# An encoder trunk whose activations are given by feature: transposes, squares of rows and reloads taken out of its first stages

## The chip, the cores and the metric

The kernel runs on one core of one Trainium2 chip. The metric is the device time of one execution in microseconds (us). The profile is one execution seen by the hardware profiler; its clock starts at the first instruction of the program. PE is the matrix engine, ACT the scalar engine, DVE the vector engine, POOL the general engine, SP the engine that issues nearly all loads and stores; a name with a q behind it (SPq) is the engine's instruction queue.

## The reference

One encoder layer over 256 tokens of width 2048, all in float32. What the change touches is the beginning:

```python
h = rms_norm(x, norm_mix_g)           # x * rsqrt(mean(x*x) + eps) * gain, along the 2048 features
proj = h @ w_in                       # feeds retention and the gated delta rule, which follow
...
mem_n = rms_norm(mem, norm_mem_g)     # 256 memory tokens of width 2048
k, v = jnp.split(mem_n @ w_kv, 2, axis=-1)   # for the cross-attention, later in the layer
```

The rest of the layer (two token mixers merged by gates, an output projection with the residual x, cross-attention into k and v, a squared-ReLU MLP, a last norm) is not changed in what it computes. Tables that depend on positions and on the decay parameters (rotations, decays per head, decays of the retention) are also computed at the start.

## The kernel before

**How a product is made.** Every weight matrix is streamed once from memory. `fetch` (line 89) loads 1 MB of it as float32 into a ring of three buffers (`raw`), rounds it on ACT in two halves to the fast matrix format (`whi`, line 108) and has DVE subtract what was rounded off (`wlo`, line 111). Both rings hold three halves. Activations are held the same way, as a rounded part and a remainder, four feature blocks of 128 to a "quad". A product is three matrix products: rounded by rounded, rounded by remainder, remainder by rounded. `chunk` (line 137) makes 256 tokens by 512 columns out of four fetches, with 96 products of 512 columns (lines 151 to 153); one half of a fetch feeds 12 of them. `blocks` (line 177) makes two blocks of 128 features by 256 tokens out of two fetches, with a pair of products (512 and 256 columns, lines 193 and 194) for each; one half of a fetch feeds eight pairs. `narrow` (line 204) makes a product of 32 columns.

**The start, in program order.** `values(0)` to `values(3)` (lines 334, 348, 377, 530, 532) are four chunks: the memory tokens by the value half of `w_xkv`. Memory is loaded in rows of tokens, four quarters of 512 features. For each quarter `load_mem` (line 325) has PE transpose sixteen 128x128 pieces two at a time into PSUM (`to_feature`, line 255, transpose on line 262) and ACT and DVE multiply by the gain and split (lines 275, 276). The scale of each token is taken from sums of squares of the rows (ACT, line 291) and multiplied in when a chunk's result is read out of PSUM (`evac_kv`, line 337). After `values(0)`, x is loaded in rows too, its squares are summed, its scale is spread over the partitions by a small product (`scale_row`, line 299), and 32 further transposes (line 364) turn it into the quads `h1`; the transposed x is also written to a scratch tensor `xt_d` (line 368), which the output projection's residual reads back. The gains come through two transposes (line 248), the convolution weights through two more (line 386). The angles for rotation (lines 402 to 428) are a chain on DVE with two table changes on ACT. After `values(2)` comes the `narrow` product, which gives the raw decays; `decay_rows` (line 455) works them up on DVE to `cl` (line 482), which is written to memory (`crow`, line 483) and read back spread over the partitions (`row`, line 509). PE transposes the rest (line 500) and DVE copies it to `bcol` (line 501). Then `decays` (line 512) makes the tables: DVE adds a mask (`em`, line 516, two buffers), ACT takes 12 exponentials of 64 columns for each pair of heads (`dec_w`, line 521), SP stores them (line 522). `ret_decays` (line 524) makes one table a head with one exponential (`dm_w`, line 526) and one store (line 527).

**The K stage.** The loop at line 539 runs `blocks` eight times over the key half of `w_xkv`; each result is multiplied by the memory scale `mrow` into `ko` (line 543) and stored. It has 32 halves of a fetch. The decay tables are made beside it. After it, the space of all these tiles is given to the mixers, which stream `w_in`.

**What sets the order.** The program is recorded in program order with priorities, and a scheduler then puts each engine's instructions in one fixed order. On the chip each engine goes through its own list strictly in order; an instruction that waits holds up all that stand behind it. Weights have a high priority, so their loads, roundings and subtractions stand early. `step` (line 80) runs one piece of a generator from the list `steps` at fixed places inside `chunk` and `blocks`; before the change only the delta rule uses it. `issue_after(i)` puts what is issued under it no earlier in the lists than instruction i.

Of the kernel before, what the change touches and what calls it, by code (L numbers as in the profile page):

```python
# [47 lines left out]
MAGIC = 1.5 * 2.0**23  # L48


@with_exitstack
def trunk(ctx: ExitStack, tc: tile.TileContext, x, mem, positions, norm_mix_g, w_in, conv_w, gdn_a_log, gdn_dt_bias,
          ret_gn_g, gdn_norm_g, w_out, norm_x_g, norm_mem_g, w_xq, w_xkv, w_xo, norm_ffn_g, w_ff1, w_ff2,
          norm_final_g, inv_freq, out):
# [21 lines left out]
    rushed = []  # L76

    fetched, steps = [], []
# [10 lines left out]
    def fetch(pieces, k, n, rush=False, hold=None, at=(0, 0)):  # L89

# [3 lines left out]
        with tc.high_priority(offset=100000):  # L94
            for off, ap in pieces:
                src = ap.rearrange("(k p) n -> p k n", p=P)
                for ks in ((slice(0, k // 2), slice(k // 2, k)) if rush else (slice(0, k),)):
                    fetched.append(nc.sync.dma_start(rv[:, ks, off:off + ap.shape[1]], src[:, ks, :]).ins)
            got = []
            for i in range(2):  # L100
# [7 lines left out]
                rounding = act.activation(hi, src, AF.Copy)  # L108
                if rush and not i:
                    rushed.append(rounding.ins)  # L110
                vec.tensor_sub(lo, src, hi.bitcast(F32))  # L111
                got.append((hi.rearrange("p (k n) -> p k n", n=n), lo.rearrange("p (k n) -> p k n", n=n)))
        return got
# [23 lines left out]
    def chunk(quads, pieces_of, evac, before=None, hold=None):  # L137

# [16 lines left out]
        for q in range(4):  # L155
            if q not in held:
                if before and q:
                    before(q)
                halves = fetch(pieces_of(q), 4, 512, rush=before is not None and q == 0)
# [66 lines left out]
    vec.memset(warm, 0.0)  # L226
    act.activation(warm, warm, AF.Exp)
    ident = cp.tile([P, P], F32, name="ident")
    ones = cp.tile([P, P], F32, name="ones")
    vec.memset(ones, 1.0)  # L230
# [9 lines left out]
    gains = cp.tile([P, 64], F32, name="gains")  # L240

    def load_gains(c0, vectors):
        rows = sm.tile([48, P], F32, name="grow", tag="junk", bufs=1)
        n = 16 * len(vectors)
        for i, g in enumerate(vectors):
            nc.sync.dma_start(rows[16 * i:16 * (i + 1), :], g.rearrange("o (k p) -> (o k) p", p=P))
        gps = bank()
        pe.transpose(gps[:, :n], rows[:n], ident[:n, :n])
        vec.tensor_copy(gains[:, c0:c0 + n], gps[:, :n])

    with tc.high_priority(offset=200000):
        load_gains(0, (norm_mem_g,))
    G_MEM, G_MIX, G_X, G_FFN = 0, 16, 32, 48

    def to_feature(src, gain, quad):

        for f2 in range(2):
# [8 lines left out]
            qh, ql = quad  # L266
            if gain is None:
                h, l = qh[:, f2 * 2:f2 * 2 + 2, :], ql[:, f2 * 2:f2 * 2 + 2, :]
                act.activation(h, pv, AF.Copy)
                vec.tensor_sub(l, pv, h.bitcast(F32))  # L270
            else:
                for f in range(2):
                    k = f2 * 2 + f
                    g = gains[:, gain + k:gain + k + 1]
                    last = act.activation(qh[:, k, :], pv[:, f, :], AF.Copy, scale=g)  # L275
                    vec.scalar_tensor_tensor(ql[:, k, :], pv[:, f, :], g, qh[:, k, :].bitcast(F32),
                                             op0=ALU.mult, op1=ALU.subtract)
        return None if gain is None else last.ins

    def rms_cols(name, ssq, count=D):  # L280

# [25 lines left out]
    def load_rows(c, src, rush, pieces=1):  # L307
        xc = kv.tile([P, NT, 512], F32, name="xc", tag="xc", bufs=8)
        rows = src[0, :, c * 512:(c + 1) * 512].rearrange("(t p) d -> p t d", p=P)
        with tc.high_priority(offset=rush):  # L310
            for ts in (slice(i * NT // pieces, (i + 1) * NT // pieces) for i in range(pieces)):
                nc.sync.dma_start(xc[:, ts, :], rows[:, ts, :])  # L312
# [812 lines left out]
```

## Time and profile before

| | us |
|---|---|
| three runs | 2080.16, 2080.26, 2081.82 (median 2080.26) |
| the profiled execution, first to last instruction | 2078.0 |
| median less that span | 2.3 |

Only the span of the profiled execution is recorded, not a time of its own; the 2.3 us beside it lie before its first and after its last instruction. Product records on PE are listed longer than the distance between their starts, since they overlap, and a PE that waits inside a stretch of products may be listed as busy. So stretches of the timeline are read by their length and the number of products in them.

### The profile page before, as it was taken

Reading aid. Unit: us, or ns where it says so; the run is one execution under the profiler, and the core shown is the slowest. Engines: PE = TensorE matmul, PEld = TensorE weight load, DVE = VectorE, ACT = ScalarE, POOL = GpSimd, SP = SyncE. Lnnn points to the kernel's source line nnn. Section 1 sums busy time; section 2 is a strip of 40 time slices with the busy share of each in tenths; the row PEclk is TensorE's granted clock in tenths of the full one; section 3 lists DMA queues with packets and bytes.
Section 4 is the critical chain, followed back from the end, with each engine's and each line's share of the span. In section 5 each row is a group of like instructions: output and inputs, shape, how many; then the busy total and the mean of one; then the engine's idle time right before and its main releaser. Section 6 shows DMA issues by size and latency. Waiting matters only on the chain.

```text
span 2078.0 us, 28543 instructions
## 1 busy us (share of the span) xinstructions
PE 2060.9 (99%) x10996; PEld 1776.8 (86%) x10996; DVE 1404.6 (68%) x2230; ACT 1115.2 (54%) x1835; POOL 30.9 (1%) x37
## 2 busy tenths in 40 slices
PE   8999999999999999999999999999999999999998
PEld 6788888888888888888888899888888888888887
DVE  5766779778757885778557665776556556645655
ACT  7584664675547554655446554654444434434444
POOL 0000000000000000000000000000000000000000
PEclk9999999999999999999999999999999999999999
DMA  8787655556555655555467664579566656556653
GB/s 300 237 274 249 197 188 195 169 177 195 187 163 190 192 181 163 190 187 191 146 213 244 190 190 153 183 204 242 185 200 185 199 185 196 188 199 186 195 190 142
DMA packets 331064, 407.21 MB, mean 196 GB/s; under 512 B 35232, under 2 KB 239024, under 8 KB 330800
## 3 DMA queue, kind: packets, MB, share of 16 engines
q1 hardware_dynamic: 330640, 404.87, 61.1%
q8 instruction: 86, 1.41, 0.3%
q10 hardware_dynamic: 288, 0.52, 0.1%
q14 instruction: 50, 0.41, 0.1%
HBM read 389.61 MB, written 13.65 MB: 194 GB/s over the span
## 4 chain that ended last, share of the span: by engine, by line
PE 95%; DMA 2%; ACT 1%; SPq 1%; DVE 1%; issue 0%; POOLq 0%; POOL 0%; ACTq 0%; DVEq 0%
PE s L193 33%; PE s L194 17%; PE s L152 13%; PE s L153 13%; PE s L151 13%; PE b L709 1%; PE b L616 1%; DMA xc<-x 1%; ACT whi L108 1%; PE b L742 1%; PE b L122 0%; PE b L121 0%; DVE wlo L111 0%; PE b L123 0%; DMA xt_d<-xt 0%; SPq L312 0%
## 5 line engine op out<-in xcount | busy, mean ns | idle before, releaser
L111 DVE TENSOR_TENSOR wlo<-raw,whi 128x1024 fp32r<-128x1024 f32 x700 | 855.5, 1223 | 510.2 <-ACT whi L108 503.8
L108 ACT ACTIVATE whi<-raw 128x1024 fp32r<-128x1024 f32 x700 | 740.6, 1059 | 688.0 <-PE s L153 338.9
L193 PE MATMUL s<-q,whi 128*128 128x512 f32 x3072 | 1056.6, 390 | 0.3 <-DVE q L1006 0.3
L194 PE MATMUL s<-q,wlo 128*128 128x256 f32 x3072 | 839.6, 281 | 0.7 <-DVE wlo L111 0.7
L193 PEld LDWEIGHTS s<-q,whi 128*128 128x128 f32 x3072 | 567.5, 188 | 109.9 <-DVE q L1006 0.5
L194 PEld LDWEIGHTS s<-q,wlo 128*128 128x128 f32 x3072 | 576.2, 188 | 14.4 <-DVE wlo L111 2.6
L152 PE MATMUL s<-wlo,q 128*128 128x512 f32 x1264 | 495.8, 392 | 0.7 <-DVE wlo L111 0.7
L153 PE MATMUL s<-whi,q 128*128 128x512 f32 x1264 | 492.1, 390 | 0.0
L151 PE MATMUL s<-whi,q 128*128 128x512 f32 x1264 | 451.2, 390 | 2.6 <-ACT q L275 2.6
L151 PEld LDWEIGHTS s<-whi,q 128*128 128x128 f32 x1264 | 237.2, 188 | 51.8 <-ACT q L275 3.0
L152 PEld LDWEIGHTS s<-wlo,q 128*128 128x128 f32 x1264 | 237.6, 188 | 49.3 <-DVE wlo L111 2.1
L153 PEld LDWEIGHTS s<-whi,q 128*128 128x128 f32 x1264 | 237.8, 188 | 47.5
L200 ACT ACTIVATE bo<-s 128x256 f32<-128x256 f32 x192 | 72.9, 379 | 121.1 <-PE s L194 107.9
L201 DVE TENSOR_TENSOR bo<-bo,s 128x256 f32<-128x256 f32 x192 | 79.9, 416 | 44.0 <-ACT bo L200 43.7
L569 DVE SCALAR_TENSOR_TENSOR acc<-bo,cw,acc 128x255 f32<-128x255 f32 (+1 forms) x144 | 66.8, 479 | 3.1 <-ACT acc L566 1.2
L678 DVE TENSOR_TENSOR pr<-lw,tw 32x31 f32<-32x31 f32 (+15 forms) x124 | 40.5, 326 | 11.1 <-DMA lw<-scr_l 9.1
L680 DVE TENSOR_TENSOR tw<-tw,pr 32x31 f32<-32x31 f32 (+15 forms) x124 | 40.6, 327 | 2.0
L843 ACT ACTIVATE gth<-s 128x512 f32<-128x512 f32 x32 | 19.0, 594 | 21.6 <-PE s L153 15.1
L1053 DVE SCALAR_TENSOR_TENSOR res<-s,rstd3q,res 128x512 f32<-128x512 f32 (+1 forms) x32 | 22.3, 735 | 12.0 <-PE s L153 12.0
L1040 DVE SCALAR_TENSOR_TENSOR hs<-bo 128x256 f32<-128x256 f32 x64 | 26.9, 421 | 1.1
L1043 DVE TENSOR_TENSOR q<-hs,q 128x256 fp32r<-128x256 f32 x64 | 26.6, 417 | 0.0
L1042 ACT ACTIVATE q<-hs 128x256 fp32r<-128x256 f32 x64 | 26.1, 409 | 0.4 <-DVE hs L1040 0.4
(304 smaller groups left out, 1075.6 us busy)
## 6 DMA issues: line engine op xcount, KB each, us to landing
raw<-w_in SPq DMA_DIRECT2D x143, 1024.0 KB
raw<-w_ff SPq DMA_DIRECT2D x128, 1024.0 KB
raw<-w_xkv SPq DMA_DIRECT2D x31, 1024.0 KB
raw<-w_out SPq DMA_DIRECT2D x16, 1024.0 KB
raw<-w_xq SPq DMA_DIRECT2D x16, 1024.0 KB
raw<-w_xo SPq DMA_DIRECT2D x16, 1024.0 KB
dec_d<-dec_w SPq DMA_DIRECT2D x8, 384.0 KB
dec<-dec_d SPq DMA_DIRECT2D x8, 384.0 KB
```

The lines of the kernel that those rows point to most:

```text
L108: rounding = act.activation(hi, src, AF.Copy)
L111: vec.tensor_sub(lo, src, hi.bitcast(F32))
L151: pe.matmul(o, xh, wh, start=first, stop=False)
L152: pe.matmul(o, xh, wl, start=False, stop=False)
L153: pe.matmul(o, xl, wh, start=False, stop=last)
L193: pe.matmul(ps[b], lh, xhl, start=kk == 0, stop=False)
L194: pe.matmul(ps[b][:, :S], ll, xh, start=False, stop=kk == KT - 1)
L200: act.activation(o, ps[b][:, S:], AF.Copy)
L201: vec.tensor_add(o, o, ps[b][:, :S])
L569: vec.scalar_tensor_tensor(acc[:, d:], ps[:, :S - d], cw[:, j, blk:blk + 1], acc[:, d:], op0=ALU.mult, op1=ALU.add)
L678: vec.tensor_mul(pv, lw[:, j, j + 1:32].unsqueeze(2).to_broadcast([32, n, j + 1]), tw[:, j, 0:j + 1].unsqueeze(1).to_broadcast([32, n, j + ...
L680: vec.tensor_sub(tw[:, j + 1:32, 0:j + 1], tw[:, j + 1:32, 0:j + 1], pv)
```

## The change

- x and memory are given as `x_f` and `mem_f`, by feature: 128 partitions, 16 feature blocks, 256 tokens. The four norm gains (`gains_f`) and a table `small_f` (convolution weights, one gain, frequencies, two decay parameters) are laid out ahead of the launch too. The 68 transposes of memory, x, gains and convolution weights fall away, and so do the store to `xt_d`; the residual reads `x_f`.
- Sums of squares are taken from features: ACT squares 128x1024 four times, DVE adds, and two products by a column of ones sum over partitions (`norm_of`). The memory scale is no longer needed in `values`; the attention multiplies it into the values it reads back, and `ko` is multiplied by it as before.
- The first fetch is cut into four loads of 256 KB and the second into two, and a load of memory of matching size stands behind each (`along`). Roundings are cut likewise.
- Eight products of ones (`WARM`) stand at the head of PE's list.
- The squares, scale and normalization of x become a generator in `steps`, run inside `values(1)` and `values(2)`; those of memory run inside `values(3)`. All are issued under `behind`, that is, no earlier than the latest load, rounding and subtraction of weights.
- The rotations move from before `values(2)` to behind `values(3)`, and the tables of the retention from the beginning into the K stage, behind the latest weights there.
- In the last gate chunk the first fetch is cut in two loads.

In the changed kernel's lists, around the decay tables: SP has a store of `dm_w` between the store of `crow` and the loads of `row`. ACT has, between the roundings of the K stage's halves 8 and 9, a table load and the sine; between 9 and 10 a table load, a `dm_w`, a table load and the cosine; between 11 and 12 a table load and 20 `dec_w`; between 12 and 13 eleven `dec_w` and the copy of the memory scale's row. DVE has `cl` behind the subtraction of half 6; two `em`, the first step of the memory scale and `bcol` between those of halves 9 and 10; one `em` behind those of halves 10 and 11, and behind 11 two `ko` also. PE has the products for the memory scale's row inside half 9. (Before: `cl` behind half 2, two `em` behind half 4, 19 `dec_w` behind half 6, no table load, and the scale's row in half 2.)

```diff
+    @contextmanager
+    def behind():
+        with ExitStack() as orders:
+            for ins in latest.values():
+                orders.enter_context(tc.issue_after(ins))
+            yield
...
-    def fetch(pieces, k, n, rush=False, hold=None, at=(0, 0)):
+    def fetch(pieces, k, n, cuts=1, along=None, hold=None, at=(0, 0)):
...
-                for ks in ((slice(0, k // 2), slice(k // 2, k)) if rush else (slice(0, k),)):
+                for c in range(cuts):
+                    ks = slice(c * k // cuts, (c + 1) * k // cuts)
                     fetched.append(nc.sync.dma_start(rv[:, ks, off:off + ap.shape[1]], src[:, ks, :]).ins)
+                    if along:
+                        along[0](ks)
...
-                rounding = act.activation(hi, src, AF.Copy)
-                vec.tensor_sub(lo, src, hi.bitcast(F32))
+                part = k * n // max(cuts, 2)
+                for c in range(0, k * n // 2, part):
+                    cs = slice(c, c + part)
+                    latest["hi"] = act.activation(hi[:, cs], src[:, cs], AF.Copy).ins
+                    if along:
+                        along[1](slice(i * k // 2 + c // n, i * k // 2 + (c + part) // n))
+                    latest["lo"] = vec.tensor_sub(lo[:, cs], src[:, cs], hi[:, cs].bitcast(F32)).ins
...
+        early = bank()
+        for _ in range(WARM):
+            pe.matmul(early[:, :P], ones, ones, start=True, stop=True)
...
+    def norm_of(name, xfs):
+        for c, xf in enumerate(xfs):
+            sq = kv.tile([P, 4, S], F32, name="sq", tag="sq" if c else "sqa", bufs=1)
+            with behind():
+                act.activation(sq, xf, AF.Square)
+                if c:
+                    vec.tensor_add(acc, acc, sq)
+                else:
+                    acc = sq
+            if c % 2:
+                yield
...
+        for t in range(NT):
+            pe.matmul(sps[:, t:t + 1], acc[:, 0, t * P:(t + 1) * P], ones[:, :1], start=True, stop=True)
...
+        rsqrt(r, s)
+        yield
+        yield r, scale_row(f"{name}_row", r)
...
+        def load(ks):
+            nc.sync.dma_start(xf[:, ks], mem_f[:, 4 * c + ks.start:4 * c + ks.stop])
+        def rounded(ks):
+            qh, ql = memq[c]
+            for k in range(ks.start, ks.stop):
+                g = gains[:, G_MEM + 4 * c + k:G_MEM + 4 * c + k + 1]
+                act.activation(qh[:, k, :], xf[:, k], AF.Copy, scale=g)
+                vec.scalar_tensor_tensor(ql[:, k, :], xf[:, k], g, qh[:, k, :].bitcast(F32), op0=ALU.mult, op1=ALU.subtract)
...
-        chunk(memq, cols(w_xkv[0], D + n * 512), evac_kv, before=load_mem if n == 0 else None)
+        chunk(memq, cols(w_xkv[0], D + n * 512), evac_kv, cuts=1 if n else 4, along=None if n else memory)
...
+        for c in range(4):
+            for k2 in range(2):
+                with behind():
+                    xn = kv.tile([P, 2, S], F32, name="xn", tag="xn", bufs=2)
+                    for f in range(2):
+                        k = 2 * k2 + f
+                        vec.scalar_tensor_tensor(xn[:, f, :], xfs[c][:, k, :], gains[:, G_MIX + 4 * c + k:G_MIX + 4 * c + k + 1], got[1], op0=ALU.mult, op1=ALU.mult)
+                    split([a[:, 2 * k2:2 * k2 + 2, :] for a in h1[c]], xn)
+                yield
...
+    steps.append(normalized())
     values(1)
...
     values(2)
+    finish_steps()
     narrow(h1, w_in[0], C_GA, 32, decay_rows)
+    steps.append(memory_norm())
     values(3)
+    finish_steps()
+    rstdm, mrow = scales
+    with behind():
+        rotations()
     row4 = [rows_of(g) for g in range(4)]
...
-        ret_decays(b2)
+        with behind():
+            ret_decays(b2)
...
-        split(vv, vr)
+        for t in range(NT):
+            r = rstdm[:, t:t + 1]
+            act.activation(vv[0][:, t], vr[:, t], AF.Copy, scale=r)
+            vec.scalar_tensor_tensor(vv[1][:, t], vr[:, t], r, vv[0][:, t].bitcast(F32), op0=ALU.mult, op1=ALU.subtract)
```

More of the change, by code (lines that the diff above doesn't have):

```diff
@@ L238, in rsqrt, with to_feature @@
         pool.tensor_tensor(o, i, nhalf_pow[:, :o.shape[1]], op=ALU.pow)
[L240 to L252, printed above, removed]
     G_MEM, G_MIX, G_X, G_FFN = 0, 16, 32, 48
-    def to_feature(src, gain, quad):
+    def to_feature(src, quad):
         for f2 in range(2):
@@ L265, in to_feature @@
                 continue
[L266 to L280, printed above, removed]
[L282 to L287 removed]
+            split([a[:, f2 * 2:f2 * 2 + 2, :] for a in quad], pv)
     def square_sum(acc, src):
@@ L548, in trunk @@
             decays(2 + b2)
-        ret_decays(b2)
+        with behind():
+            ret_decays(b2)
     kvs.close()
```

225 lines of the change are left out of this document (101 added, 124 removed).

## The prediction

> **What bounds the kernel now.** I read the page first, then the stretches of the timeline cut at the first product of each stage, then the timeline of the first 20 us, and last the chain of work that ended last with the lists of ACT, DVE and SP around the decay tables.
>
> ```profile
> span 2078.0 us, 28543 instructions
> PE 2060.9 (99%) x10996; PEld 1776.8 (86%) x10996; DVE 1404.6 (68%) x2230; ACT 1115.2 (54%) x1835; POOL 30.9 (1%) x37
> PE 95%; DMA 2%; ACT 1%; SPq 1%; DVE 1%; issue 0%; POOLq 0%; POOL 0%; ACTq 0%; DVEq 0%
> ```
>
> PE is the bound from end to end: only what takes time out of PE's list, or out of its waits, counts. In the order of the lists, the changed kernel differs from before only in the start and the K stage, but for a cut load and the scaled values in the attention. So I ask stage by stage how far each is from pure products. The stretches, first with the products of the weight stream alone, then with PE's other work alone (start and end, length, busy time and number on PE, ...):
>
> ```profile
> 9.94:36.51 26.57, 24.12 (x97) 18.46 (x97) 0.00 (x0) 0.24 (x1) 0.00 (x0) 1.00 0.96 337
> 36.51:61.06 24.55, 22.62 (x97) 17.79 (x96) 0.00 (x0) 1.57 (x3) 0.00 (x0) 1.00 0.83 277
> 61.06:86.11 25.05, 23.45 (x98) 17.53 (x96) 0.00 (x0) 1.37 (x3) 0.00 (x0) 1.00 0.70 226
> 89.79:112.04 22.25, 22.08 (x98) 17.95 (x97) 6.79 (x14) 0.87 (x2) 0.00 (x0) 1.00 0.66 201
> 112.04:203.67 91.63, 89.78 (x514) 77.78 (x513) 5.83 (x14) 6.27 (x17) 0.00 (x0) 1.00 0.83 267
> 203.67:220.25 16.58, 16.58 (x99) 14.66 (x98) 1.62 (x4) 1.37 (x4) 0.00 (x0) 1.00 0.78 253
> 1455.95:1477.74 21.79, 21.79 (x98) 18.03 (x97) 1.12 (x3) 0.62 (x2) 0.00 (x0) 1.00 0.58 193
> ```
> ```profile
> 9.94:36.51 26.57, 3.70 (x24) 3.49 (x24) 7.28 (x16) 6.53 (x15) 1.00 0.96 337
> 36.51:61.06 24.55, 2.17 (x17) 2.00 (x17) 1.85 (x5) 1.34 (x3) 1.00 0.83 277
> 61.06:86.11 25.05, 3.33 (x22) 2.70 (x22) 5.56 (x14) 3.47 (x6) 1.00 0.70 226
> 112.04:203.67 91.63, 1.45 (x10) 1.10 (x10) 0.26 (x1) 0.38 (x1) 1.00 0.83 267
> ```
>
> An undisturbed chunk of 96 products takes 21.79 us (last row of the first block; counts include neighbours at the edges): 0.227 us a product, 2.72 for a half fetch. Six halves of `blocks` take 16.58: 2.76 a half. Against this, `values(0)` to `values(3)` take 26.57, 24.55, 25.05 and 22.25, and the K stage 91.63 where 32 halves need 88.4. The excess is 4.8, 2.8, 3.3, 0.5 and 3.2 us; before the first product stand 9.94 us. That is all there is to win: some 24 us, of which a first load cannot be avoided.
>
> **The first stage: the head.**
>
> ```profile
> 1.24 0.89 SPq L312 DMA_DIRECT2D xc<-mem  x2
> 4.45 0.69 PE L262 MATMUL b<-ident,xc 128*128 128x128 f32 x2 [1.74 <-DMA xc<-mem]
> 5.75 1.54 PE L262 MATMUL b<-ident,xc 128*128 128x128 f32 x6 [0.62 <-DMA xc<-mem]
> 8.47 1.06 ACT L108 ACTIVATE whi<-raw 128x1024 fp32r<-128x1024 f32 x1 [5.39 <-DMA raw<-w_xkv]
> 9.43 0.82 ACT L275 ACTIVATE q<-b,gains 128x256 fp32r<-128x256 f32 x2
> 9.56 1.23 DVE L111 TENSOR_TENSOR wlo<-raw,whi 128x1024 fp32r<-128x1024 f32 x1 [6.64 <-ACT whi L108]
> 9.94 1.22 PE L151 MATMUL s<-whi,q 128*128 128x512 f32 x2 [2.65 <-ACT q L275]
> 10.70 0.87 DVE L276 SCALAR_TENSOR_TENSOR q<-b,gains,q 128x256 fp32r<-128x256 f32 x2
> ...
> 13.04 11.95 DMA xc<-x
> ```
>
> The landings give the pace of loading. Issue of the first big load at 1.24; then 0.26 MB had landed at 4.45, 0.52 at 5.75, 1.05 at 8.47, and with the last load of x (13.04 + 11.95 = 24.99) 7.34 MB: 6.29 MB in 16.5 us, 0.381 MB/us. In the changed kernel the first weights are issued at the start of SP's list, 0.45 us earlier, and need no transpose. I keep the landings by bytes. First pair of pieces (0.39 MB) at about 4.6, first product at 5.1 in place of 9.94. Until the third quarter PE lives from hand to mouth, so that neither the pace of its early products nor the eight warm-up products, which stand in idle time, count. The third quarter decides: weights (4.2 MB in all) land at 16.2, memory (4.7 MB) at 17.6. ACT's list has both roundings ahead of memory's: 16.2 + 2 x 1.0 + 0.41 = 18.6 for the first product. DVE's list has both subtractions first: 17.2 + 2 x 1.2 + 0.43 = 20.0 for the third product of the first feature block. PE is through with that block at 20.5 and with the quarter (18 x 0.227) at 24.6. The fourth quarter's loads (6.3 MB) land at 21.8 and are split in time, so `values(0)` ends at 24.6 + 5.45 = 30.0, not 36.51: **-6.5 us**.
>
> **values(1) and values(2).** Their 32 transposes of x, two of gains and two of convolution weights go; left are two one-column products and four for the row. Ten small products cost 1.45 above, 0.15 each. So 21.8 + 0.3 = 22.1 and 21.8 + 0.6, plus 0.2 for small waits such as `values(3)` has today: 22.6. **-2.4 and -2.4 us**. Their weights come in time: behind the first fetch (24.5) stand 2.1 MB of x (30.0), then the next fetch (32.8), which PE needs at 35.5. `narrow` and `values(3)`: 0, since squares of memory on ACT (four of about 1 us) lie beside 22 us of products.
>
> Costed at nothing: the values' scaling in the attention (two half-size instructions for one, DVE and ACT at 68% and 54%); the reads of `x_f` for `xt_d`; the tables by small loads; the cut last gate fetch. If their cover were gone they would cost under 0.5 us together, by the sizes of the rows above.
>
> **The K stage gives some back.** Here the lists matter. A ring of three halves lets a subtraction end 2 x 2.76 - 1.06 - 1.23 = 3.2 us later than it could before PE waits.
>
> ```profile
> 41.79 1.28 ACT L425 ACT_TABLE_LOAD   x1
> 43.08 0.42 ACT L425 ACTIVATE sin<-ang 128x256 f32<-128x256 f32 x1
> 53.93 0.71 POOL L238 TENSOR_TENSOR n_r<-n_s,nhalf_pow 128x2 f32<-128x2 f32 x1 [24.33 <-DVE n_s L284]
> 112.59 4.96 DMA crow<-cl
> 117.59 3.96 DMA row<-crow
> 119.38 1.06 ACT L108 ACTIVATE whi<-raw 128x1024 fp32r<-128x1024 f32 x1 [1.91 <-PE s L193]
> 122.61 2.01 ACT L521 ACTIVATE dec_w<-em,bcol 128x64 f32<-128x64 f32 x8
> 126.20 1.05 ACT L108 ACTIVATE whi<-raw 128x1024 fp32r<-128x1024 f32 x1
> 128.55 0.50 PE L194 MATMUL s<-q,wlo 128*128 128x256 f32 x2 [0.34 <-DVE wlo L111]
> 121.64 1.29 DVE L516 TENSOR_TENSOR em<-row,trimask 128x512 f32<-128x512 f32 x2 [2.79 <-DMA row<-crow]
> 122.86 1.22 DVE L111 TENSOR_TENSOR wlo<-raw,whi 128x1024 fp32r<-128x1024 f32 x1
> 130.15 0.42 DVE L543 TENSOR_TENSOR ko<-bo,mrow 128x256 f32<-128x256 f32 x1
> ```
>
> Today 19 exponentials (0.24 each) stand between two roundings, which lie 6.8 us apart, and PE waits a little. With the small products, that makes the 3.2 us of excess: 1.6 of products, 1.6 of waits. In the changed kernel the tables come about four halves later, among table loads. Let PE end half 6 of the stage at 0. ACT rounds half 9 until 1.1, then table load, `dm_w`, table load, cosine: 4.3; halves 10 and 11 until 6.5; table load, 7.8. On SP the store of that `dm_w` stands ahead of the loads of `row`, so these go at 3.2, though `crow` has long been written; they land 4.0 later, at 7.2. DVE, with two `em` ahead of the subtraction of half 10, waits for that: `em` 8.5, memory scale and `bcol` 8.7, subtraction 9.9. POOL's power ends at 9.4; PE, which reached the row's products in half 9 at 8.2, has **waited 1.2**. The exponentials begin with `bcol`: 20 until 13.5, half 12 rounded at 14.5. DVE's fourth `em` needs the first one's buffers, that is 24 exponentials: 15.4 to 16.0; two `ko` need the scale's row, copied by ACT at 16.7: 17.6; subtraction of half 12: 18.8. PE is there at 16.9: **1.9**. Followed on the same way, half 14 is 0.7 late and half 16 0.9; then the exponentials thin out. Waits of 4.7 for 1.6, and two more small products: **+3.3 us**.
>
> The sum is -6.5 - 2.4 - 2.4 + 3.3 = -8.0 us: a span of 2070.0. With the 2.3 us by which the median stands above the profiled span: **2072.3 us**.
>
> **The rivals.**
>
> *The K stage gets no worse* (the lists run looser than I follow them, or the loads of `row` land sooner): without the +3.3, 2069.0. For it: today DVE idles 2.79 us for the same load without a wait on PE. Against: three table loads of 1.28 are new there.
>
> *Small pieces load badly.* Were the first 3.15 MB, all that is cut, to land at 0.2 MB/us, the distance of the first two landings today (0.26 MB in 1.3 us), the loads would end at 4.0 + 2.89 / 0.2 + 3.15 / 0.381 = 26.7, not 21.8; the head would gain 1.6, and the time be 2077.2. Against: those two landings lie in the ramp. The Trainium skill ("SBUF — State Buffer", "The DMA setup-cost knee") says that a transfer has a fixed cost of about 2 us whatever its size, and advises the largest single transfers; by it twelve pieces one after another would take an estimated 24 us of fixed cost and this stage would gain nothing. The trace disagrees for pieces in flight together: the second landed 1.3 us behind the first.
>
> *x comes late.*
>
> ```profile
> L371 DVE SCALAR_TENSOR_TENSOR xn<-b,gains,rrow 128x256 f32<-128x256 f32 x16 | 6.8, 476 | 4.1 <-ACT xt L367 4.1
> L375 DVE TENSOR_TENSOR q<-xn,q 128x512 fp32r<-128x512 f32 x7 | 4.7, 683 | 0.0
> ```
>
> In `values(2)` DVE has, per half, a subtraction of 1.22, two such multiplications (6.8 / 16 each) and one of 0.68: 2.75 against PE's 2.72. No slack is regained; crossings with ACT of 0.4 us in each of seven halves would cost 2.8: 2075.1.
>
> *Slower: weights behind ACT's stores.*
>
> ```profile
> 28.80 5.47 DMA raw<-w_xkv
> 124.64 4.19 SPq L522 DMA_DIRECT2D dec_d<-dec_w  x2
> 128.92 0.43 SPq L98 DMA_DIRECT2D raw<-w_xkv  x1
> ```
>
> In SP's list of the K stage eight fetches stand behind stores that wait for exponentials. A fetch takes 5.5 us to land, 1.0 to round, 1.2 to subtract: 7.7 against the 5.5 that PE takes to use it up. In my reckoning each is issued 3 to 8 us before it must be. From 3 us more delay on ACT, the fetches would come one by one, eight times 2.2 = 17.6 us: 2089.9. For it: the wait for a store ahead of a fetch is there today, 4.19 us. Against: the slack.
>
> **How the numbers follow.** Forecast 0.52, no worse K stage 0.22, small pieces 0.10, x late 0.09, slower 0.07. The predicted time is 2072.3. The unknown sizes are the landings (1 us either way), and the K stage's waits (from none added to twice my 3.3). Low: 2069.0 less 1 = 2068.0. High: 2072.3 + 3.3 + 1 = 2076.6. This leaves out small pieces, slower, and edges of the others: 0.2. A measurement of this kernel tells apart about 0.2%, 4.2 us: faster means below 2076.1. Forecast, first and third rival mostly lie there (0.78); 2077.2 is no change (with edges 0.15); slower 0.07.
>
> **What would show it.** First weight product at about 5 us; first product of `values(1)` at 30, of `values(2)` at 52, of `narrow` at 75; K stage 95 us long with waits of PE for `wlo` and for the memory scale's row around its halves 9 to 16, DVE idle before `em` for `row`. A later end of `values(0)` with PE waiting for loads speaks for small pieces; waits in `values(2)` for `wlo`, or of `narrow` for x, for the third rival; PE waiting in the K stage with ACT idle for `raw`, for the fourth. Anything that changes beyond 250 us would be outside this account.

## The result, and the profile after

The changed kernel takes **2073.78 us**, median of five runs (2073.39 to 2074.12), beside 2080.31 for the kernel before (2080.16 to 2082.83): a ratio of 0.9965, interval 0.9953 to 0.9978, so 0.35% less time. The forecast was 2072.3, its range 2068.0 to 2076.6. The profiled execution has a span of 2072.1 us in place of 2078.0.

The stretches of the timeline of the changed kernel, cut at the first product of each stage as in the prediction, the products of the weight stream alone (start and end, length, then busy time and number on PE, PEld, DVE, ACT and POOL, the granted clock, the DMA share and GB/s): `values(0)`, `values(1)`, `values(2)`, `narrow`, `values(3)`, the K stage and the first six halves of `w_in`.

```profile
4.97:30.18 25.21, 24.18 (x96) 18.20 (x97) 0.00 (x0) 0.03 (x1) 0.00 (x0) 1.00 1.02 390
30.18:53.03 22.85, 22.65 (x98) 17.96 (x97) 0.00 (x0) 1.65 (x3) 0.00 (x0) 1.00 0.78 262
53.03:75.86 22.83, 22.63 (x97) 17.90 (x96) 0.00 (x0) 1.07 (x2) 0.00 (x0) 1.00 0.61 189
75.86:79.56 3.70, 3.70 (x18) 2.41 (x17) 0.00 (x0) 0.68 (x2) 0.00 (x0) 1.00 0.67 251
79.56:102.36 22.80, 22.64 (x98) 17.74 (x96) 3.52 (x6) 0.88 (x2) 0.00 (x0) 1.00 0.65 196
102.36:196.77 94.41, 91.14 (x513) 77.87 (x512) 8.78 (x23) 5.76 (x17) 0.00 (x0) 1.00 0.85 271
196.77:214.02 17.25, 16.89 (x99) 14.59 (x98) 1.61 (x4) 1.38 (x4) 0.00 (x0) 1.00 0.72 236
```

| us | forecast | measured |
|---|---|---|
| start and `values(0)`, 36.51 to | -6.5 | -6.33 (30.18) |
| `values(1)`, 24.55 to | -2.4 | -1.70 (22.85) |
| `values(2)`, 25.05 to | -2.4 | -2.22 (22.83) |
| `narrow` | 0 | 0.02 |
| `values(3)`, 22.25 to | 0 | +0.55 (22.80) |
| K stage, 91.63 to | +3.3 | +2.78 (94.41) |
| six halves of `w_in`, 16.58 to | 0 | +0.67 (17.25) |
| the rest of the span | 0 | +0.3 |
| span | -8.0 | -5.9 |

The first weight product starts at 4.97 (5.1 was forecast), and `values(1)` and `values(2)` have lost their transposes. But `values(3)` and the halves of `w_in`, whose work is nearly the same, are longer, and `values(1)` and `(2)` are longer than their 96 products and few small ones should be. `values(3)` shows what it is, since nearly nothing but products stands in it. In the chain of work of the kernel before, three starts twelve products apart; then the same in the changed kernel:

```profile
92.69 0.45 PE s L151 x2
95.41 0.45 PE s L151 x2
98.13 0.45 PE s L151 x2
```
```profile
88.10 0.47 PE s L162 x2
90.90 0.47 PE s L162 x2
93.70 0.47 PE s L162 x2
```

2.72 us for twelve products before, 2.80 after: 0.227 and 0.233 each, without a wait, at a granted clock of 1.00 in both. **PE itself goes through the same products 3% slower**, in all four value stages and, by 1%, in the K stage (2.79 us a half for 2.76). That is 96 x 0.006 = 0.6 us in each of `values(1)` to `(3)` and, summed over all intervals between neighbouring products of the K stage that hold no wait, 0.9 there: 2.7 us. In `values(0)`, which waits for loads, it is mostly hidden.

In the K stage the waits forecast are there. The timeline of the changed kernel, SP first, then ACT, DVE, POOL and PE:

```profile
115.31 0.34 SPq L437 DMA_DIRECT2D crow<-cl  x1
119.50 0.36 SPq L481 DMA_DIRECT2D dm_d<-dm_w  x1
119.91 1.40 SPq L463 DMA_DIRECT2D row<-crow  x3
117.67 1.28 ACT L480 ACT_TABLE_LOAD   x1
118.97 0.51 ACT L480 ACTIVATE dm_w<-dist,lnk 128x256 f32<-128x256 f32 x1
126.82 0.59 ACT L475 ACTIVATE dec_w<-em,bcol 128x64 f32<-128x64 f32 x2 [1.61 <-DVE bcol L455]
125.26 1.29 DVE L470 TENSOR_TENSOR em<-row,trimask 128x512 f32<-128x512 f32 x2 [1.85 <-DMA row<-crow]
126.70 1.78 POOL L255 TENSOR_TENSOR nm_r<-nm_s,nhalf_pow 128x2 f32<-128x2 f32 x1 [72.87 <-DVE nm_s L308]
128.54 0.71 PE L286 MATMUL b<-ident,nm_r 128*128 128x128 f32 x4 [0.63 <-POOL nm_r L255]
133.97 0.50 PE L205 MATMUL s<-q,wlo 128*128 128x256 f32 x2 [0.29 <-DVE wlo L122]
137.82 0.50 PE L205 MATMUL s<-q,wlo 128*128 128x256 f32 x2 [0.53 <-DVE wlo L122]
140.87 0.47 PE L204 MATMUL s<-q,whi 128*128 128x512 f32 x1 [0.46 <-DVE bo L212]
```

PE waits four times here: for the memory scale, twice for `wlo`, once for `bo`. The idle times in brackets are short of the loss, since a product is listed beyond the start of the next: by the starts of neighbouring products the four cost 0.8, 0.5, 0.7 and 0.6 us. Behind it all DVE waits for `row`, which lands 5.3 us after its issue at 119.91.

### The profile page after: what moved, and what is told of

Read it like the earlier page. It is cut to its first block, busy times and chain, and to the rows that moved or that the text cites. A ratio compares the mean times of both kernels' runs of the same rounds, so it can differ in the third digit from the quotient of the medians.

```text
span 2072.1 us, 28404 instructions
## 1 busy us (share of the span) xinstructions
PE 2059.2 (99%) x10952; PEld 1772.2 (86%) x10952; DVE 1412.0 (68%) x2240; ACT 1113.3 (54%) x1811; POOL 30.3 (1%) x37
## 4 chain that ended last, share of the span: by engine, by line
PE 97%; DMA 1%; ACT 1%; DVE 1%; issue 0%; SPq 0%; POOLq 0%; POOL 0%; DVEq 0%; ACTq 0%
PE s L204 33%; PE s L205 17%; PE s L163 14%; PE s L164 14%; PE s L162 14%; DMA raw<-w_xkv 1%; PE b L703 1%; PE b L610 1%; PE b L736 1%; PE b L134 0%; PE b L133 0%; PE b L135 0%; ACT dec_w L475 0%; DVE wlo L122 0%; ACT whi L119 0%
## 5 line engine op out<-in xcount | busy, mean ns | idle before, releaser
L122 DVE TENSOR_TENSOR wlo<-raw,whi 128x1024 fp32r<-128x1024 f32 (+1 forms) x702 | 856.0, 1220 | 512.2 <-ACT whi L119 504.9
L119 ACT ACTIVATE whi<-raw 128x1024 fp32r<-128x1024 f32 (+1 forms) x702 | 741.2, 1057 | 692.8 <-PE s L164 358.3
L563 DVE SCALAR_TENSOR_TENSOR acc<-bo,small,acc 128x255 f32<-128x255 f32 (+1 forms) x144 | 66.8, 480 | 3.1 <-ACT acc L560 1.2
L837 ACT ACTIVATE gth<-s 128x512 f32<-128x512 f32 x32 | 18.9, 592 | 17.6 <-PE s L164 15.2
```

The costliest lines, as they stand in the source:

```text
L119: latest["hi"] = act.activation(hi[:, cs], src[:, cs], AF.Copy).ins
L122: latest["lo"] = vec.tensor_sub(lo[:, cs], src[:, cs], hi[:, cs].bitcast(F32)).ins
L563: vec.scalar_tensor_tensor(acc[:, d:], ps[:, :S - d], cw[:, j, blk:blk + 1], acc[:, d:], op0=ALU.mult, op1=ALU.add)
```

## The experiments

All are the changed kernel but for the lines shown, unless said otherwise. Ratios are to the kernel before, run beside each. With the changed kernel a run is compared by the lengths of its stages first, since runs of one kernel spread over up to 3 us (the kernel before: 3.6).

The stages vary too, and each was profiled once for each kernel. Where a run leaves them as they are, `values(0)` ended at 29.28 to 30.56 (six traces with the changed kernel's first loads and warm-up products), the K stage took 93.61 to 94.41 (six traces with the same lists there), and all that follows the first six halves of `w_in`, the same in all thirteen traces but for a load and the values' scaling, took 1857.8 to 1859.3. A difference within such a spread is not put down to the lines that were changed unless something else shows it.

**1. Is the slower pace one of place?** The change takes small tiles out of the constants, so that all tiles behind them stand 64 bytes lower in each partition, but memory's operand tiles, in a pool of their own, only 32. Their distance to the weights' rings has thus grown by 32 bytes. A pad ahead of them sets it.

```
-PAD1, PAD2 = 144, 80
+PAD1, PAD2 = 136, 80
```

> The changed kernel with memory's four operand tiles 32 bytes lower in each partition (the pad ahead of them 136 numbers long, not 144); nothing else differs. In the changed kernel the 512-column products on memory's tiles follow each other in 0.232 to 0.233 us, those on x's tiles and all of the kernel before in 0.227. Theory (the place of memory's tiles, which the change moved by 32 bytes against the weights' buffers, makes the slower pace): the products of values(0) to values(3) and of the K stage come at 0.227, values(3) falls from 22.8 to 22.3 us, the four value stages and the K stage lose about 3.2 us together, and the time is about 2070.6. Rival (the slower pace belongs to the first 200 us, by the clock or by the load on the memory): 2073.8, pace unchanged.

Measured 2071.77 (2071.27 to 2073.24), ratio 0.9958, interval 0.9944 to 0.9971. The value stages (again cut at first products):

```profile
30.13:52.35 22.22, 22.02 (x97) 17.95 (x96) 0.00 (x0) 1.66 (x3) 0.00 (x0) 1.00 0.85 282
52.35:74.64 22.29, 22.09 (x98) 17.90 (x96) 0.00 (x0) 1.07 (x2) 0.00 (x0) 1.00 0.61 185
78.32:100.63 22.31, 22.14 (x97) 17.74 (x96) 3.45 (x6) 0.86 (x2) 0.00 (x0) 1.00 0.66 203
100.63:195.53 94.90, 91.39 (x513) 78.14 (x512) 8.85 (x23) 5.81 (x17) 0.00 (x0) 1.00 0.86 269
```

`values(1)`, `(2)` and `(3)` lose 0.6, 0.5 and 0.5 us: their products are back at 0.227. `values(0)` ends at 30.13, no sooner, since loads decide there. The K stage did not follow: 94.90. In the chain of work its halves begin like this, early and late in the stage:

```profile
106.34 0.46 PE s L204 x2
109.10 0.46 PE s L204 x2
111.87 0.46 PE s L204 x2
...
150.61 0.46 PE s L204 x2
153.42 0.46 PE s L204 x2
156.23 0.46 PE s L204 x2
```

2.77 us a half at first, as before the change; 2.81 from the wait at 139 us on, first on the same tiles, then in `w_in` until about 207. So in this stage the distance is not the whole of it: here the pace changed at an interruption and then stayed. What sets it was not found.

**2. The converse: the distance alone, in the kernel before.**

```
-PAD1, PAD2 = 144, 80
+PAD1, PAD2 = 152, 80
```

> The kernel before with memory's operand tiles 32 bytes higher (pad 152 numbers long, not 144): the distance to the weights' buffers that the changed kernel has, and nothing else of the change. Theory (that distance makes the slower pace of the value stages): 512-column products in values(1) to values(3) at 0.233 in place of 0.227, each of the three stages 0.5 to 0.6 us longer (values(3) 22.25 to 22.8), values(0) longer by as much or less, the K stage by 0.9 if it follows, time 2082.3 to 2083.5. Rival (the pace of the changed kernel comes from its order or its loads): values(3) 22.25, time 2080.3.

Measured 2082.45 (2081.48 to 2083.7, ten runs) beside 2080.31: ratio 1.0008, interval 0.9999 to 1.0017. The time alone would not settle it; the stages do. `values(3)` and the K stage:

```profile
90.70:113.53 22.83, 22.66 (x98) 17.95 (x96) 6.79 (x14) 0.87 (x2) 0.00 (x0) 1.00 0.64 197
113.53:206.18 92.65, 90.64 (x513) 77.70 (x512) 5.84 (x14) 6.25 (x17) 0.00 (x0) 1.00 0.84 264
```

22.83 for 22.25 and 92.65 (2.79 a half) for 91.63, with nothing of the change in the kernel. `values(0)` took 27.87 for 26.57; `values(1)` stayed at 24.55 and `values(2)` lost 0.3, though their products too came at 0.233: these stages wait for other things. The distance makes the slow pace of the value stages, both ways.

**3. The place or the distance?** A tile of 32 bytes ahead of all others moves everything and changes no distance.

```
+    cp.tile([P, 8], F32, name="shift")
```

> The changed kernel with every tile 32 bytes higher in each partition (a tile of 32 bytes at the front); no distance between two tiles changes. If the pace of the products goes by the distance between an operand tile and the weights' buffers, nothing changes: 0.233 in values, 0.2315 in the K stage, 0.227 beyond 203 us, time 2073.8. If it goes by the place of the operand tile itself (fast at 32 beyond a multiple of 64, slow at a multiple of 64), values and K become fast (3 us less) and every weight stream on x's tiles slow: 0.231 to 0.233 for 0.227, 2% of some 1700 us, time 2095 to 2115. If it goes by the weights' place, a mixture: values slow or fast against the streams by blocks.

Measured 2073.3 (2071.43 to 2073.4). `values(3)` 22.80, all value stages at 0.233, and the streams on x's tiles beyond 210 us at 0.227 as in the changed kernel. In the value stages it is the distance. The stages that wait for landings moved although nothing in their lists had: `values(0)` ended at 29.28, with the second quarter's rounding begun at 9.78 in place of 10.56, and the K stage took 93.61.

**4. Do the rotations and decays make the waits of the K stage?** Both parts as they were before the change: the rotation tables computed ahead of `values(2)`, the retention decays free of `behind()`.

```
+    rotations()
     values(2)
...
-    with behind():
-        rotations()
...
-        with behind():
-            ret_decays(b2)
+        ret_decays(b2)
```

> The changed kernel with the rotation tables computed ahead of values(2) and the retention decays no longer tied behind the latest weights, as the kernel before has both: sine, cosine and all eight dm_w leave ACT's list in the K stage, their stores leave SP's. Theory (in the K stage the table loads and the store of dm_w ahead of the loads of row make the waits): the loads of row go about 4 us sooner, the waits of PE around halves 9 to 16 fall from 3.6 us to about 1.6, the K stage from 94.4 to about 92.4, and the time to about 2071.8. Rival (the exponentials and the memory scale alone make the waits): 2073.8 within 0.5, K stage 94 or more. Against both: work that now stands in values(1) and values(2) makes these stages longer by up to 1.

Measured 2071.68 (2070.46 to 2073.44), ratio 0.9959, interval 0.9946 to 0.9971. Then each part alone: the retention decays free, and the rotations early.

> The changed kernel with only the retention decays no longer tied behind the latest weights: all eight dm_w leave the K stage, with their two table loads on ACT and their stores on SP; sine and cosine stay in it. Theory A (the store of dm_w ahead of the loads of row, and with it ACT's table loads around that dm_w, makes the added waits): the loads of row go about 4 us sooner, K stage 92 to 92.4, time 2071.4 to 2071.8, all of what undoing both brought. Theory B (sine, cosine and their table load make them): K stage 93.5 to 94.4, time 2073 to 2073.8.

Measured 2073.03 (2072.47 to 2074.2), ratio 0.9962, interval 0.9949 to 0.9974.

> The changed kernel with only the rotation tables ahead of values(2) (20 instructions on DVE, two sines and their table load on ACT); the retention decays stay tied behind the latest weights. Untying these alone left the loads of row at 119.5 us, though no store stood ahead of them; undoing both brought them to 113.8. Theory (the loads of row wait for crow, and crow is late because the rotations' instructions stand ahead of the decays' sums on DVE): crow stored at about 111, loads of row at 114 to 115 though the dm_w are tied as in the changed kernel, K stage 92 to 93, time 2071.7 to 2072.7. Rival (the stores of dm_w hold the loads back once they are there): loads of row at 117 or later, K stage 93.5 or more, time 2073 to 2073.8.

Measured 2072.41 (2071.52 to 2072.6), ratio 0.9957, interval 0.9945 to 0.997. The K stage with both, with the decays alone, with the rotations alone:

```profile
102.25:194.05 91.80, 90.48 (x514) 77.84 (x512) 8.64 (x21) 6.01 (x17) 0.00 (x0) 1.00 0.84 267
```
```profile
102.30:195.62 93.32, 91.12 (x513) 77.86 (x512) 8.86 (x23) 5.89 (x17) 0.00 (x0) 1.00 0.82 262
```
```profile
102.74:195.68 92.94, 91.15 (x514) 77.85 (x512) 8.53 (x21) 5.87 (x17) 0.00 (x0) 1.00 0.86 275
```

94.41 falls by 2.6, 1.1 and 1.5. Beside the 93.61 to 94.41 of the K stages that were left as they are, the 2.6 is clear (1.8 below the shortest) and the 1.5 fairly so (0.7 below), while the 1.1 of the freed decays is hardly more than the spread (0.3 below). That the two parts add up is therefore not shown; what is shown is that theory A of the second run fails, for the stage stays 0.9 above its 92.4.

SP's list tells what each does. With the decays free:

```profile
115.25 0.35 SPq L437 DMA_DIRECT2D crow<-cl  x1
119.51 1.78 SPq L463 DMA_DIRECT2D row<-crow  x4
```

With the rotations early:

```profile
111.49 0.34 SPq L437 DMA_DIRECT2D crow<-cl  x1
115.27 1.31 SPq L463 DMA_DIRECT2D row<-crow  x3
```

Without any store in between, the loads of `row` still go at 119.51, 4.3 us behind the store of `crow`; in the changed kernel it is 4.6, in the kernel before 5.0 (112.59 to 117.59). They wait for `crow` to land; the store to `dm_d` adds 0.4 us (119.91 in the changed kernel). What brings them forward is `crow` itself, 3.8 us sooner once the rotations' instructions no longer stand ahead of the decays' sums on DVE.

With the free decays `row` lands 1.1 us sooner (`em` starts at 124.12 for 125.26): the fourth of its loads no longer stands behind a fetch, but goes with the others by 121.29 (in the changed kernel at 121.84). Much of that is no more than chance, though: in the six K stages that were left as they are, with the first of these loads issued at the same 17.6 us from the stage's start, `em` began anywhere from 22.1 to 22.9 us behind it, and in the two shortest of them, as with the free decays (21.8), PE waits under 0.2 us for the memory scale, where the changed kernel's trace has 0.8. Of four table loads on ACT in this stage two are left; what these were worth was not taken apart. Not all is won: with the rotations early `values(2)` takes 23.29 for 22.83 and `values(1)` 22.40 for 22.85, since products and work of theirs only change places.

**5. What do the small first pieces bring?** The first loads whole:

```
-        chunk(memq, cols(w_xkv[0], D + n * 512), evac_kv, cuts=1 if n else 4, along=None if n else memory)
+        chunk(memq, cols(w_xkv[0], D + n * 512), evac_kv, cuts=1, along=None if n else memory)
```

> The changed kernel with the first two quarters of values(0) loaded in whole pieces (weights of 1.05 MB, memory of 0.52 MB) and rounded in halves, as the later ones are. Theory (the landing of the third quarter decides when values(0) ends; the cuts only bring the first product forward): first product at about 8 us in place of 5.0, the third quarter's first product still at 18.4 to 19.4, end of values(0) 30.2 to 31.2, time 2073.8 to 2074.8. Rival (the cuts bring the head's gain): the end of values(0) moves as the first product does, by 3 us, to 33, time 2076.8. Second rival (small pieces load badly): the later quarters land sooner, end of values(0) below 30, time below 2073.5.

Measured 2076.37 (2075.48 to 2077.36, eleven runs), ratio 0.998, interval 0.9972 to 0.9989. First product at 9.02, end of `values(0)` at 34.10: 3.9 us later, nearly as much as the first product. (The time is only 2.6 longer: the K stage, 93.77, and the halves of `w_in`, 16.96, came out 0.9 shorter in this trace, within their spread.) The theory fails here; its rival has the size, but the reason is another. Two-microsecond stretches of the timeline (columns as above, all instructions):

```profile
6.00:8.00 2.00, 0.00 (x0) 0.00 (x0) 0.35 (x1) 1.44 (x2) 0.00 (x0) 0.97 1.00 339
8.00:10.00 2.00, 0.98 (x2) 0.84 (x3) 2.00 (x3) 2.00 (x5) 0.00 (x0) 0.50 1.05 393
10.00:12.00 2.00, 2.00 (x6) 1.59 (x5) 1.73 (x6) 1.22 (x2) 0.00 (x0) 0.50 1.03 410
12.00:14.00 2.00, 2.00 (x6) 1.54 (x6) 2.00 (x4) 1.71 (x4) 0.00 (x0) 0.50 1.06 409
```

PE stands idle from the last warm-up product to the first weights, 4.3 us, and the granted clock drops to 0.50 (at 7.90 us, until 14.72); 13 products then take 0.427 each. That is a reason of its own, which could be taken away:

```
-WARM = 8
+WARM = 26
...
-        chunk(memq, cols(w_xkv[0], D + n * 512), evac_kv, cuts=1 if n else 4, along=None if n else memory)
+        chunk(memq, cols(w_xkv[0], D + n * 512), evac_kv, cuts=1, along=None if n else memory)
```

> The run with whole first loads (end of values(0) 34.1, first product 9.0) with 26 warm-up products in place of 8, which fill TensorE's idle time up to the first product. There the granted clock was 0.50 from 8 to 14 us and 13 products took 0.427 each, behind 4.3 us of idle TensorE. Theory (the idle time costs the clock, and the clock costs the 2.7 us): clock 1.00, first product at 9.0, products at 0.233 from the first, end of values(0) at 31.4 to 31.8, time about 2073.7. Rival (the whole loads themselves cost it): end of values(0) at 34, time 2076.4.

Measured 2075.45 (2074.54 to 2076.05), ratio 0.9973, interval 0.9961 to 0.9985. `values(0)` with its 96 products:

```profile
9.18:31.90 22.72, 22.72 (x96) 18.04 (x97) 0.00 (x0) 0.50 (x1) 0.00 (x0) 1.00 1.04 404
```

It ends at 31.90, just past the theory's 31.8: of the 3.9 us, 2.2 were the clock's, 1.7 those of the later first product. The forecast time, 2073.7, did not follow: the median fell by 0.9 only, and in this trace what follows the first halves of `w_in` took 0.85 us longer, again within its spread. From 9.18 on PE is hardly ever short of data again: with whole loads the later quarters are in time, and the late start is all there is.

**6. Do the warm-up products count, in the changed kernel?**

```
-WARM = 8
+WARM = 0
```

> The changed kernel without the eight warm-up products ahead of the first weights. Theory of the prediction (PE lives from hand to mouth until the third quarter, whose landing decides): early products slow at the lower clock, which is granted for about 5.5 us of products (behind the idle time with whole loads it was 0.50 up to 14 us), third quarter still from 18.4 us on, end of values(0) 30.2 to 30.7, time 2073.8 to 2074.3. Rival (the lower clock makes PE late for good): 13 products at 0.427 for 0.233 put the third quarter back by 1.5 to 2.5 us, end of values(0) 31.7 to 32.7, time 2075.3 to 2076.3.

Measured 2073.12 (2072.97 to 2073.17), ratio 0.9961, interval 0.9947 to 0.9975. The first stretch and the stretch in which the pace changes (PE alone: busy, number; clock; DMA):

```profile
6.00:8.00 2.00, 2.00 (x6) 1.00 0.95 329
8.00:10.00 2.00, 2.00 (x6) 1.00 0.98 349
10.00:12.00 2.00, 2.00 (x9) 1.00 1.05 396
```

Six products in 2 us are the slow pace, 0.427 each up to 10.4 us. But the third quarter begins at 18.96 for 18.36, and `values(0)` ends at 30.29 for 30.18. With small pieces PE has nothing to hurry for until the third quarter has landed. It has nothing more to lose either: in this run it goes from the first product to the end of the stage all but without a wait (12 products at 0.427, one between the two paces and 83 at 0.233 make 24.8 of its 25.1 us), so the slow products have just used up the waits that the changed kernel has there. And the eight products do not keep the whole start at full pace in the changed kernel: there the full clock is granted at 6.35 us only, and the first three products of weights are slow as well.

**7. Does the third quarter decide?** It is cut in two as the second is.

```
-                halves = fetch(pieces_of(q), 4, 512, cuts=max(cuts >> q, 1), along=along(q) if along else None)
+                halves = fetch(pieces_of(q), 4, 512, cuts=(4, 2, 2, 1)[q] if along else max(cuts >> q, 1),
+                               along=along(q) if along else None)
```

> The changed kernel with the third quarter of values(0) loaded and rounded in two pieces, as the second is. Theory (the third quarter's landing and its roundings, both weights ahead of memory, set the end of values(0)): its first product comes up to 1 us sooner than 18.4, the wait of 0.4 in its middle goes, end of values(0) 29.2 to 29.8, time 2072.8 to 2073.4. Rival (the pace of all landings, or the second quarter, sets it): end 30.2 within 0.3, time 2073.8.

Measured 2072.45 (2071.87 to 2074.35), ratio 0.9959, interval 0.9947 to 0.9972. The third quarter's first product stays at 18.33, but the wait inside it is gone. The stage, and then the third quarter alone, in the changed kernel and in this run:

```profile
4.91:29.53 24.62, 23.85 (x96) 18.57 (x97) 0.00 (x0) 0.03 (x1) 0.00 (x0) 1.00 1.03 387
```
```profile
18.36:24.58 6.22, 5.97 (x24) 4.54 (x25) 0.00 (x0) 0.00 (x0) 0.00 (x0) 1.00 1.04 410
18.33:23.93 5.60, 5.60 (x25) 4.51 (x24) 0.00 (x0) 0.00 (x0) 0.00 (x0) 1.00 1.04 404
```

The end comes at 29.53, 0.65 sooner. By itself that would lie within the spread, but the quarter takes 5.60, its 24 products and nothing else, for 6.15 to 6.22 in the six traces with the changed kernel's first loads and warm-up products. The order "both weights, then memory" on ACT and DVE was worth 0.6. The quarter could not begin sooner, since PE comes to it straight from the second quarter here, without a wait: so the second quarter sets its start.

**8. What gained, together**: pad 136, rotations and decays early, third quarter in two.

> The changed kernel with the three edits that gained alone: memory's operand tiles at their old distance (pad 136), rotation tables and retention decays early, third quarter in two pieces. If the gains are separate: values(0) ends at 29.5 less what the faster pace gives behind the third quarter (some 0.3), values(1) and (2) at 22.2 to 22.7, values(3) 22.3, K stage 91 to 92, time 2068.5 to 2069.5. If the faster pace only turns into waits for the same loads and rows: about 2070.5.

Measured **2070.09** (2069.15 to 2070.22), ratio 0.9945, interval 0.9932 to 0.9959. `values(0)`, `values(1)` and the K stage:

```profile
4.93:28.56 23.63, 22.87 (x96) 17.82 (x97) 0.00 (x0) 0.03 (x1) 0.00 (x0) 1.00 1.03 383
28.56:51.87 23.31, 22.34 (x98) 17.87 (x96) 0.00 (x0) 1.06 (x2) 0.00 (x0) 1.00 0.96 324
100.58:192.76 92.18, 90.37 (x514) 77.77 (x512) 8.69 (x22) 6.00 (x17) 0.00 (x0) 1.00 0.83 266
```

It is faster than the changed kernel by 3.7 us. Alone, the three had brought 2.0, 2.1 and 1.3, together 5.4, so the time lies nearer to the second forecast (gains turn into waits) than to the first. `values(0)` ends 1.6 us sooner than in the changed kernel, but `values(1)` gives 0.5 back: its second fetch of weights, behind 2 MB of x in SP's list, is now the thing that PE waits for. In the K stage the halves stay at 2.77 us and less, but for the waits: the slower pace that came up within run 1 did not come back.

## Why the prediction was right

**The head: right, by its own steps.** The third quarter decided: its first product was forecast for 18.6 and came at 18.36, the third product of its first feature block for 20.0 and came at 19.81, the end of the quarter for 24.6 (24.58), of the stage for 30.0 (30.18). (The end lay anywhere from 29.3 to 30.6 in six traces with this head, so that it came within 0.2 is luck.) That the early pace and the warm-up products do not count is shown by run 6. What the account did not say is why the small pieces were needed: run 5 with its lower clock.

**values(1) and values(2): right, a size off.** Their transposes are gone; the 0.7 and 0.2 us that are missing are the slower pace, 0.6 each, less, in `values(2)`, 0.4 of small products and waits that were allowed for and did not come.

**values(3): the step that failed.** "`narrow` and `values(3)`: 0" rested on the products' pace being a constant, 0.227. It is one of two or more, and the change moved memory's tiles by 32 bytes against the rings. I read the pace from the trace of before and never asked what set it; the pad that stands ahead of these very tiles in the code was a sign.

**The K stage: size right by luck, one reason of it wrong.** +3.3 was forecast, +2.78 measured, but 0.9 of it is the pace, and the waits grew by half of what was forecast. They were to be 1.2 for the memory scale's row and 1.9, 0.7 and 0.9 behind it, 4.7 in all, for 1.6 before; by the starts of the products they were 0.8, 0.5, 0.7 and 0.6, 2.6 in all, for two of 0.5 before. Small products and the gaps beside them make the remaining 0.3. The line of waits came as forecast (`row`, `em`, the memory scale, `wlo`): counted from the rounding at 116.6 ahead of the `dm_w`, the loads of `row` were to go 3.2 us later and went 3.3, though their landing took 5.3 for 4.0. But the step behind that number, "on SP the store of that `dm_w` stands ahead of the loads of `row`, so these go at 3.2, though `crow` has long been written", is wrong. `crow` had not been written: it was stored at 115.31, and its landing released the loads at about the moment when the store was issued too. Two things ended at the same 119.5, and I had followed one.

**w_in: missed, and a matter of a landing.** Of its +0.67, one wait of PE for `wlo` is 0.5. DVE's timeline of the changed kernel:

```profile
203.99 1.03 DVE L551 MEMSET pair<- 128x512 f32 x2 [2.04 <-DMA kt_d<-ko]
...
207.63 2.28 DVE L122 TENSOR_TENSOR wlo<-raw,whi 128x1024 fp32r<-128x1024 f32 x2
```

DVE clears the mixers' tiles only when the last store of the K stage has landed, and the subtractions stand behind that. That store is issued 3.3 us after the first product of `w_in` in all thirteen traces. The clearing begins 5.8 and 5.9 us after that product in the two traces of the kernel before, and 5.8 to 7.2 in the eleven of the changed kernel and its variants; where it begins by 6.7 PE does not wait, at 7.2 it waits 0.5. In seven of the ten variants the stretch takes 16.6 to 17.0, in three 17.1 to 17.2. The run without warm-up products, with the same lists here, took 16.62, as the kernel before does. So this term is one landing of 2.5 to 4.0 us. Why it is mostly longer after the change than before is open.

**The rivals.** Small pieces that load badly (2077.2) did not come: the third quarter was there on time. Nor did x late, or weights behind ACT's stores. "K no worse" did not come either, though half of what it is worse by is not what I said.

**The sum: right in part by luck.** The section on the time before has 2.3 us lie before the first and after the last instruction, and the sum adds them to the span. They do not lie there. Wherever time and span of one run are recorded together, for either kernel, they differ by 1.7 us (2.05 at most); a run of the kernel before of 2080.31 has a span of 2078.6. So by its span of 2078.0 the profiled execution was some 0.6 us quicker than the median run. From span to span -8.0 was forecast and -5.9 came, a miss of 2.1; the time missed by 1.5 only because the wrong 2.3 stood in the sum. The slower pace, 2.7 us, was not in the sum at all, and 1.5 of waits that stayed away in the K stage covered more than half of it.

## What to carry to other kernels

Where PE is the bound, take the time of a product from the trace of the kernel at hand, and check after each change of memory layout whether it still holds: a few constants fewer can move operands against each other. An order that puts early work "behind the latest weights" frees the head, but moves everything that hangs on it, here 17 small instructions on DVE (5.3 us by their listed times) ahead of a store and a load that take 10 us from issue to landing. And when a queue's order and a landing both end at the same moment, ask which would be late if the other went. Before a microsecond is put down to a change, look how far the same stage moves in runs that leave it as it is.

## What the runs showed of the hardware

- Back-to-back products of 512 columns have more than one pace at a granted clock of 1.00: 0.227 us, 0.233 in the value stages whenever memory's operand tiles stand 32 bytes further from the weights' rings, and in the K stage 2.76, 2.79 and 2.81 us for a half. In one run the pace changed at a wait in the K stage and held for nearly 70 us, into `w_in`. No column of the profile shows it; only the starts do.
- 4.3 us of idle PE cost half the clock for 5.5 us of products: 0.427 us each. Without warm-up products the same slow products come from 5.15 to 10.4 us, though the clock column reads 1.00 there: the first record of the clock in that trace stands at 10.71 us. The pace is the surer sign.
- In the nine runs with eight warm-up products, which begin at 1.10 us, the full clock was granted at 4.12 to 7.03 us, that is, 3.0 to 5.9 us after the first of them. The Trainium skill ("TensorE: Matmul & The Clock Gate", "Part 1: The HAM clock gate (the "warmup" mystery)") gives 426.7 ns for 512 columns at half clock, which the trace agrees with, and about 3.4 us of sustained work until it is lifted, by a window that runs free of the kernel's start, where these runs show 3.0 to 5.9.
- The same loads and stores, issued at the same distance from a stage's start, land up to 1.4 us apart from one trace to another: the loads of `row` by 0.8, the last store of the K stage by 1.4, as told by the start of what waits for them.
